# Interleaving two tensors: nine tiles of 28.5 KiB rows with three output buffers, in place of eight tiles of 32 KiB rows with two

## The chip, the core and the metric

The kernel runs on one core of a Trainium2 chip. A core has engines that run side by side, each with its own queue of instructions: here VectorE (DVE) copies, while SyncE (SP) and ScalarE (ACT) only issue DMA transfers. Sixteen DMA engines move data between the chip's large memory (HBM) and the core's own memory (SBUF), which has 128 partitions. Engines wait for one another by semaphores. The metric is the time of one execution on the device, in microseconds (us).

## The reference

```python
batch, seq, dim = 32, 256, 1024          # x, y: float32
result = np.zeros((batch, seq, dim * 2), dtype=np.float32)
result[..., 0::2] = x
result[..., 1::2] = y
```

The output takes its elements from x and y by turns. Nothing is computed: 33.55 MB of each input are read and 67.11 MB are written.

## The kernel before

The inputs are seen as flat arrays and cut into 8 tiles of 128 rows, each row 8192 float32 (32 KiB), one row to a partition. A tile of x and one of y give an output tile of 128 rows of 64 KiB; it is made and stored in two halves (h = 0 and 1), each 128 rows of 32 KiB. SBUF holds two buffers of x (xt), two of y (yt) and two for output halves (ot), all of 32 KiB a partition.

- *Loads* (L42 to L53) are issued by SP. The first tile of x comes as two halves with semaphores of their own (L42, L43), and these two DMAs are moved into the program's opening block, ahead of the common start (L103 to L122). Then come, tile by tile, x (L50) and y (L53). From the third tile on, the load of x waits (L48) until the third of the four copies of the tile two back is done, which is the last that reads that x buffer, and the load of y (L52) until the fourth is done.
- *Copies* (L55 to L70) are done by DVE, four a tile: for each half, x into the even places of the output buffer (L67), then y into the odd places (L70). The x copy waits for the tile's x and, from the second tile on, for the store that last used this output buffer (L64). The first y copy of a tile waits for y (L69). Each copy adds one to the semaphore `woven`.
- *Stores* (L72 to L85) are issued by ScalarE, each when its half has both copies. The first half is stored in two pieces, the first quarter (L77) and the rest (L81), all others as one DMA of 4096 KB (L83).
- *The end* (L87 to L93): ScalarE waits for the stores of output buffer 0 and clears the semaphores; SP waits for those of buffer 1, the last of which is the last store, and resets that semaphore.

Order is fixed by the program text on each of the three queues; between queues the semaphores alone decide. Loads and stores are separate DMA queues (q1 and q10 in the profile) that share the same sixteen engines.

Of the kernel before, what the change touches and what calls it, by code (L numbers as in the profile page):

```python
# [3 lines left out]


def _interleave(nc, x, y, out):
    P = 128
    W = 8192
    H = W // 2  # L10

    total = 1
    for s in x.shape:
        total *= s
    n = total // (P * W)
    assert n * P * W == total

    def rows(ap, names, k):
        flat = ap.rearrange("b s d -> (b s d)")
        return flat[k * names : (k + 1) * names].rearrange("(p w) -> p w", p=P)  # L20

    fp32 = mybir.dt.float32
    xt = [nc.alloc_sbuf_tensor(f"xt{b}", [P, W], fp32).ap() for b in (0, 1)]
    yt = [nc.alloc_sbuf_tensor(f"yt{b}", [P, W], fp32).ap() for b in (0, 1)]
    ot = [nc.alloc_sbuf_tensor(f"ot{b}", [P, W], fp32).ap() for b in (0, 1)]

    xsem = [nc.alloc_semaphore(f"xsem{b}") for b in (0, 1)]
    hsem = nc.alloc_semaphore("hsem")
    qsem = nc.alloc_semaphore("qsem")
    ysem = [nc.alloc_semaphore(f"ysem{b}") for b in (0, 1)]  # L30
    woven = nc.alloc_semaphore("woven")
    osem = [nc.alloc_semaphore(f"osem{b}") for b in (0, 1)]


    cuts = [0, W // 4, W]
    parts = [slice(a, b) for a, b in zip(cuts, cuts[1:])]

    xs = [rows(x, P * W, k) for k in range(n)]
    ys = [rows(y, P * W, k) for k in range(n)]
    os_ = [rows(out, 2 * P * W, k) for k in range(n)]  # L40

    nc.sync.dma_start(out=xt[0][:, :H], in_=xs[0][:, :H]).then_inc(xsem[0], 16)  # L42
    nc.sync.dma_start(out=xt[0][:, H:], in_=xs[0][:, H:]).then_inc(hsem, 16)  # L43

    for k in range(n):
        b = k % 2
        if k >= 2:
            nc.sync.wait_ge(woven, 4 * (k - 2) + 3)  # L48
        if k:
            nc.sync.dma_start(out=xt[b], in_=xs[k]).then_inc(xsem[b], 16)  # L50
        if k >= 2:
            nc.sync.wait_ge(woven, 4 * (k - 2) + 4)  # L52
        nc.sync.dma_start(out=yt[b], in_=ys[k]).then_inc(ysem[b], 16)  # L53

    for k in range(n):  # L55
        b = k % 2
        for h in (0, 1):
            c = slice(h * H, (h + 1) * H)
            if h == 0:
                nc.vector.wait_ge(xsem[b], 16 * (k // 2 + 1))  # L60
            elif k == 0:
                nc.vector.wait_ge(hsem, 16)
            if k:
                nc.vector.wait_ge(osem[h], 16 * k)  # L64
            if (k, h) == (1, 0):
                nc.vector.wait_ge(qsem, 16)
            nc.vector.tensor_copy(out=ot[h][:, 0::2], in_=xt[b][:, c]).then_inc(woven, 1)  # L67
            if h == 0:
                nc.vector.wait_ge(ysem[b], 16 * (k // 2 + 1))  # L69
            nc.vector.tensor_copy(out=ot[h][:, 1::2], in_=yt[b][:, c]).then_inc(woven, 1)  # L70

    for k in range(n):  # L72
        for h in (0, 1):
            nc.scalar.wait_ge(woven, 4 * k + 2 * h + 2)
            if (k, h) == (0, 0):
                for c in parts[:-1]:
                    nc.scalar.dma_start(  # L77
                        out=os_[k][:, c], in_=ot[h][:, c]
                    ).then_inc(qsem, 16)
                c = parts[-1]  # L80
                nc.scalar.dma_start(out=os_[k][:, c], in_=ot[h][:, c]).then_inc(osem[h], 16)  # L81
                continue
            nc.scalar.dma_start(  # L83
                out=os_[k][:, h * W : (h + 1) * W], in_=ot[h]
            ).then_inc(osem[h], 16)  # L85

    nc.scalar.wait_ge(osem[0], 16 * n)  # L87
    used = sorted(s.num for s in [*xsem, hsem, qsem, *ysem, woven, osem[0]])
    assert used == list(range(used[0], used[-1] + 1)), used
    nc.scalar.sem_clear(range(used[0], used[-1] + 1))  # L90
    nc.sync.nop(nofuse=True).wait_op(osem[1], 16 * n, "sem-ge").then_inc(
        osem[1], -16 * n
    )  # L93


def kernel(tc, x, y, out):
    nc = tc.nc
    tc.close()
    tc.compile()

    _interleave(nc, x, y, out)

    blocks = nc.main_func.blocks  # L103
    for engine in (mybir.EngineType.SP, mybir.EngineType.SP):
        opening = blocks[0].instructions
        at, moved = next(
            (b, i)
            for b in blocks[1:]
            for i in b.instructions
            if i.engine == engine and i.opcode == "DMACopy"  # L110
        )
        assert not (moved.sync_info and moved.sync_info.on_wait)
        body = at.instructions
        body.remove(moved)
        gate = next(
            n
            for n, i in enumerate(opening)
            if i.engine == engine and i.opcode == "Drain"
        )
        opening.insert(gate, moved)  # L120
        at.instructions = body
        blocks[0].instructions = opening  # L122


# [1 line left out]
_INS = ['x', 'y']  # L126
_OUTS = [((32, 256, 2048), 'float32')]


# [23 lines left out]
```

## Time and profile before

| what | us |
|---|---|
| time, median of 3 runs (314.10 to 314.26) | 314.18 |
| the profiled execution: span | 312.9 |
| DVE busy, 32 copies | 72.0 |
| one copy, 128x4096 | 2.29 |
| DVE waiting for stores | 206.5 |
| DVE waiting for y, once, and for x, once | 12.3 and 7.3 |
| store of 4096 KB, issue to landing, median | 34.1 |
| load of y, 4096 KB, issue to landing, median | 41.5 |

The span is the time from the first to the last event of one profiled execution, to which the other rows belong. The times of the runs are a little longer, since they hold what lies around the span; the span is 312.86 us in the trace, 1.32 us less than the median. Time to landing runs from the issuing instruction to the completion of the transfer, with all the time that it stands behind other transfers.

The profile names lines of the kernel (L67), engines (SPq and ACTq are the queues from which SP and ScalarE issue DMAs) and tiles without buffer numbers (ot for ot0 and ot1). A DMA packet is what one engine moves as one piece.

### The profile page before, as it was taken

The page shows a single profiled execution, that of the slowest core. Times are in us where ns is not written, and L with a number is a line of the kernel's source. Part 1 is how long each engine was busy: PE and PEld are TensorE (multiplying, and loading weights), DVE is VectorE, ACT ScalarE, POOL GpSimd, SP SyncE. Part 2 cuts the span into 40 slices and gives each one's busy share as a digit, 9 for nine tenths or more (in the row PEclk, how much of TensorE's full clock was granted, in tenths as well). Part 3 has the DMA queues.
Part 4 walks back from the last instruction along what each step waited for, and adds up shares of the span by engine and source line. Part 5 has one row for each costly group of instructions (what it writes and reads, how often), then busy time and mean ns, then how long its engine had stood idle before and what let it go on. Part 6 is the DMA issues. An engine that isn't in the chain of part 4 may idle for free.

```text
span 312.9 us, 114 instructions
## 1 busy us (share of the span) xinstructions
DVE 72.0 (23%) x32; POOL 0.2 (0%) x4
## 2 busy tenths in 40 slices
DVE  0216000501305023050220503205032050415410
POOL 0000000000000000000000000000000000000000
DMA  8999999999999999999999999999999999999998
GB/s 337 467 402 436 436 402 419 452 457 415 427 444 411 461 402 469 402 469 402 469 402 465 406 440 432 423 448 402 469 402 469 402 469 402 469 402 448 423 423 381
DMA packets 4896, 134.22 MB, mean 429 GB/s; under 512 B 544, under 2 KB 544, under 8 KB 544
## 3 DMA queue, kind: packets, MB, share of 16 engines
q1 hardware_dynamic: 2448, 67.11, 50.1%
q10 hardware_dynamic: 2448, 67.11, 49.7%
HBM read 67.11 MB, written 67.11 MB: 429 GB/s over the span
## 4 chain that ended last, share of the span: by engine, by line
DMA 82%; DVE 12%; issue 0%
DMA out_dram<-ot 76%; DMA yt<-in_y_dram 6%; DVE ot L70 6%; DVE ot L67 6%
## 5 line engine op out<-in xcount | busy, mean ns | idle before, releaser
L67 DVE COPY ot<-xt 128x4096 f32<-128x4096 f32 x16 | 36.7, 2295 | 213.8 <-DMA out_dram<-ot 206.5
L70 DVE COPY ot<-yt 128x4096 f32<-128x4096 f32 x16 | 36.6, 2288 | 12.3 <-DMA yt<-in_y_dram 12.3
L137 POOL MEMSET const-bfloat16-1.0<- 128x1 bf16 x1 | 0.1, 103 | 0.0
L137 POOL MEMSET const-uint8-127<- 128x1 uint8 x1 | 0.1, 102 | 0.0
L137 POOL MEMSET const-float32-0.0<- 128x1 f32 x1 | 0.1, 100 | 0.2 <-issue 0.2
L137 POOL MEMSET const-float32-1.0<- 128x1 f32 x1 | 0.1, 99 | 0.0
## 6 DMA issues: line engine op xcount, KB each, us to landing
out_dram<-ot ACTq DMA_DIRECT2D x15, 4096.0 KB, 34.1
yt<-in_y_dram SPq DMA_DIRECT2D x8, 4096.0 KB, 41.5
xt<-in_x_dram SPq DMA_DIRECT2D x7, 4096.0 KB, 24.3
xt<-in_x_dram SPq DMA_DIRECT2D x2, 2048.0 KB, 9.5
out_dram<-ot ACTq DMA_DIRECT2D x1, 3072.0 KB, 32.8
out_dram<-ot ACTq DMA_DIRECT2D x1, 1024.0 KB, 16.3
```

The lines of the kernel that those rows point to most:

```text
L67: nc.vector.tensor_copy(out=ot[h][:, 0::2], in_=xt[b][:, c]).then_inc(woven, 1)
L70: nc.vector.tensor_copy(out=ot[h][:, 1::2], in_=yt[b][:, c]).then_inc(woven, 1)
L137: nc = _bacc.Bacc("TRN2", target_bir_lowering=False, num_devices=1)
```

## The change

The tiles become nine: eight with rows of 7296 elements (28.5 KiB) and a ninth with rows of 7168 (28 KiB). The buffers have 28.5 KiB a partition; x and y keep two each, and the output has three. Output halves are numbered j = 2k + h over all tiles and use buffer j % 3, so a copy waits for the store three halves back (`osem[j % O]`) and not for the one two halves back. The first x load is still cut in two halves, now of 14592 bytes a row, and the first store in a quarter and the rest, now 7296 and 21888 bytes a row. The waits of the loads keep their counts. At the end ScalarE waits for the two output semaphores that don't belong to the last store, and SP for the third.

```diff
-    W = 8192
-    H = W // 2
+    WIDTHS = [7296] * 8 + [7168]
+    W = max(WIDTHS)
+    O = 3
...
-    ot = [nc.alloc_sbuf_tensor(f"ot{b}", [P, W], fp32).ap() for b in (0, 1)]
+    ot = [nc.alloc_sbuf_tensor(f"ot{b}", [P, W], fp32).ap() for b in range(O)]
...
+    half = WIDTHS[0] // 2
+    nc.sync.dma_start(out=xt[0][:, :half], in_=xs[0][:, :half]).then_inc(xsem[0], 16)
+    nc.sync.dma_start(out=xt[0][:, half : 2 * half], in_=xs[0][:, half:]).then_inc(hsem, 16)
...
-    for k in range(n):
+    for k, w in enumerate(WIDTHS):
         b = k % 2
         if k >= 2:
             nc.sync.wait_ge(woven, 4 * (k - 2) + 3)
         if k:
-            nc.sync.dma_start(out=xt[b], in_=xs[k]).then_inc(xsem[b], 16)
+            nc.sync.dma_start(out=xt[b][:, :w], in_=xs[k]).then_inc(xsem[b], 16)
...
+            j = 2 * k + h
+            c = slice(h * w // 2, (h + 1) * w // 2)
+            woven_to = ot[j % O]
             if h == 0:
                 nc.vector.wait_ge(xsem[b], 16 * (k // 2 + 1))
             elif k == 0:
                 nc.vector.wait_ge(hsem, 16)
-            if k:
-                nc.vector.wait_ge(osem[h], 16 * k)
-            if (k, h) == (1, 0):
+            if j >= O:
+                nc.vector.wait_ge(osem[j % O], 16 * (j // O))
+            if j == O:
                 nc.vector.wait_ge(qsem, 16)
-            nc.vector.tensor_copy(out=ot[h][:, 0::2], in_=xt[b][:, c]).then_inc(woven, 1)
+            nc.vector.tensor_copy(out=woven_to[:, 0:w:2], in_=xt[b][:, c]).then_inc(woven, 1)
             if h == 0:
                 nc.vector.wait_ge(ysem[b], 16 * (k // 2 + 1))
-            nc.vector.tensor_copy(out=ot[h][:, 1::2], in_=yt[b][:, c]).then_inc(woven, 1)
+            nc.vector.tensor_copy(out=woven_to[:, 1:w:2], in_=yt[b][:, c]).then_inc(woven, 1)
...
+            j = 2 * k + h
+            first = 0
+            nc.scalar.wait_ge(woven, 2 * j + 2)
+            if j == 0:
+                first = w // 4
+                nc.scalar.dma_start(out=os_[k][:, :first], in_=ot[0][:, :first]).then_inc(
+                    qsem, 16
+                )
             nc.scalar.dma_start(
-                out=os_[k][:, h * W : (h + 1) * W], in_=ot[h]
-            ).then_inc(osem[h], 16)
+                out=os_[k][:, h * w + first : (h + 1) * w], in_=ot[j % O][:, first:w]
+            ).then_inc(osem[j % O], 16)
...
+    for b in range(O):
+        if b != last:
+            nc.scalar.wait_ge(osem[b], done[b])
```

In the changed file, which is 10 lines longer, the x copy is L72, the y copy L75, the loads of x and y L53 and L56, and the stores L84 (the first quarter) and L87 (all others).

More of the change, by code (lines that the diff above doesn't have):

```diff
@@ L14, in _interleave, with tiles @@
         total *= s
-    n = total // (P * W)
-    assert n * P * W == total
-    def rows(ap, names, k):
+    n = len(WIDTHS)
+    assert sum(WIDTHS) * P == total
+    def tiles(ap, names):
         flat = ap.rearrange("b s d -> (b s d)")
-        return flat[k * names : (k + 1) * names].rearrange("(p w) -> p w", p=P)
+        cut, made = 0, []
+        for w in WIDTHS:
+            end = cut + names * P * w
+            made.append(flat[cut:end].rearrange("(p w) -> p w", p=P))
+            cut = end
+        return made
     fp32 = mybir.dt.float32
@@ L31, in _interleave @@
     woven = nc.alloc_semaphore("woven")
[L32 to L43, printed above, removed]
-    for k in range(n):
+    osem = [nc.alloc_semaphore(f"osem{b}") for b in range(O)]
+    xs = tiles(x, 1)
+    ys = tiles(y, 1)
+    os_ = tiles(out, 2)
+    half = WIDTHS[0] // 2
+    nc.sync.dma_start(out=xt[0][:, :half], in_=xs[0][:, :half]).then_inc(xsem[0], 16)
+    nc.sync.dma_start(out=xt[0][:, half : 2 * half], in_=xs[0][:, half:]).then_inc(hsem, 16)
+    for k, w in enumerate(WIDTHS):
         b = k % 2
@@ L69, in _interleave @@
                 nc.vector.wait_ge(ysem[b], 16 * (k // 2 + 1))
-            nc.vector.tensor_copy(out=ot[h][:, 1::2], in_=yt[b][:, c]).then_inc(woven, 1)
-    for k in range(n):
+            nc.vector.tensor_copy(out=woven_to[:, 1:w:2], in_=yt[b][:, c]).then_inc(woven, 1)
+    for k, w in enumerate(WIDTHS):
         for h in (0, 1):
[L74 to L82, printed above, removed]
-            nc.scalar.dma_start(
-                out=os_[k][:, h * W : (h + 1) * W], in_=ot[h]
-            ).then_inc(osem[h], 16)
@@ L87, in _interleave @@
-    nc.scalar.wait_ge(osem[0], 16 * n)
-    used = sorted(s.num for s in [*xsem, hsem, qsem, *ysem, woven, osem[0]])
+            j = 2 * k + h
[6 more added lines that the diff above has]
+                )
+            nc.scalar.dma_start(
+                out=os_[k][:, h * w + first : (h + 1) * w], in_=ot[j % O][:, first:w]
+            ).then_inc(osem[j % O], 16)
@@ L89, in _interleave @@
+    stores = 2 * n
+    last = (stores - 1) % O
+    done = [16 * len(range(b, stores, O)) for b in range(O)]
+    for b in range(O):
+        if b != last:
+            nc.scalar.wait_ge(osem[b], done[b])
+    clear = [s for b, s in enumerate(osem) if b != last]
+    used = sorted(s.num for s in [*xsem, hsem, qsem, *ysem, woven, *clear])
     assert used == list(range(used[0], used[-1] + 1)), used
     nc.scalar.sem_clear(range(used[0], used[-1] + 1))
-    nc.sync.nop(nofuse=True).wait_op(osem[1], 16 * n, "sem-ge").then_inc(
-        osem[1], -16 * n
+    nc.sync.nop(nofuse=True).wait_op(osem[last], done[last], "sem-ge").then_inc(
+        osem[last], -done[last]
```

5 lines of the change are left out of this document (2 added, 3 removed).

## The prediction

> **What bounds the kernel now.** I read the page's first three parts, then the chain of waits, the table of waits, the timeline, and last the windows by stage. DVE (VectorE) is the only compute engine in use, and it is not the bound:
>
> ```profile
> span 312.9 us, 114 instructions
> ...
> DVE 72.0 (23%) x32; POOL 0.2 (0%) x4
> ...
> DMA  8999999999999999999999999999999999999998
> ...
> DMA packets 4896, 134.22 MB, mean 429 GB/s; under 512 B 544, under 2 KB 544, under 8 KB 544
> ...
> q1 hardware_dynamic: 2448, 67.11, 50.1%
> q10 hardware_dynamic: 2448, 67.11, 49.7%
> ```
>
> The two queues' packets took 50.1% + 49.7% = 99.8% of the span on all sixteen DMA engines. So the engines are never idle between the first packet and the last one. The packet count also shows how a transfer is cut: 34 DMAs x 16 engines = 544 tiny completion packets, and the other 4352 are 34 x 128, one per row of a tile. So each engine does 8 row packets and one completion packet per DMA, 306 in all.
>
> ```profile
> DMA 82%; DVE 12%; issue 0%
> ```
>
> ```profile
> 81.36 34.17 DMA out_dram<-ot
> 115.53 0.02 issue
> 115.55 2.29 DVE ot L67
> 117.85 2.21 DVE ot L70
> 120.06 0.02 issue
> 120.08 34.17 DMA out_dram<-ot
> ```
>
> ```profile
> DVE ot L67 <- DMA out_dram<-ot: 206.5, 14, 29.0
> ```
>
> These are the page's chain, a stretch of the chain in order of time (start, length, what), and the first line of the waits (total, times, longest). DVE stood 206.5 us for output buffers, which a reader could take for a shortage of them. It is not: a store takes 34.17 us to land only because it shares full engines with the loads. The chain repeats every 120.08 - 81.36 = 38.72 us; windows over three such periods (length, DVE, POOL, clock, DMA share, GB/s) say what the engines do meanwhile:
>
> ```profile
> 41.00:79.70 38.70, 7.37 (x4) 0.00 (x0) 1.00 1.00 434
> ...
> 118.40:157.10 38.70, 8.97 (x5) 0.00 (x0) 1.00 1.00 434
> ...
> 195.80:234.60 38.80, 9.06 (x5) 0.00 (x0) 1.00 1.00 432
> ```
>
> The DMA share is 1.00 in each, at 432 to 434 GB/s. The end is as full, as the timeline's last copies but one show:
>
> ```profile
> 283.90 2.30 DVE L67 COPY ot<-xt 128x4096 f32<-128x4096 f32 x1 [8.95 <-DMA out_dram<-ot]
> ...
> 293.53 2.29 DVE L67 COPY ot<-xt 128x4096 f32<-128x4096 f32 x1 [5.14 <-DMA out_dram<-ot]
> ```
>
> Both copies were released by a store's landing, 9.63 us apart, with stores alone in flight: 4096 KB in 9.63 us is 435.5 GB/s. Loads mixed with stores and stores alone run at one rate.
>
> **What a packet costs.** The trace's single packet records, which the page only sums, took 309 ns for 8192 B, 611 for 16384, 912 for 24576 and 1213 for 32768: 301.3 ns for each 8 KiB, that is 27.2 GB/s per engine or 435 for sixteen, and a fixed part. The fixed part follows from the period: 38.72 us hold, per engine, 32 rows of 32 KiB (32 x 1205.2 = 38.57 us) and 36 packets in all, so 0.15 us / 36 = 4.2 ns a packet. The records' own remainder, 8 ns, is the upper bound, since records overlap a little. All bytes at 435 GB/s take 134.22 MB / 435 = 308.5 us, and 306 packets x 4.2 ns = 1.3 us: 309.8 of the 312.9 us. What is left, 3.1 us, is the first microsecond (16 GB/s in the window 0 to 1 us) and slow packets at two places: summed over an engine, 0.6 us in the first 3 us and 0.55 us between 26 and 41 us, when the first stores begin.
>
> **The change part by part.** The bytes stay. Everything else is counted against these 312.9 us and the 1.3 us by which the runs' median, 314.18 us, stands above this span; nothing in the change touches what lies outside the span, since SP's closing wait is still for the last store alone and ScalarE's wait for the other two output semaphores ends earlier.
>
> *More, shorter transfers.* Loads go from 17 to 19 and stores from 17 to 19: 38 DMAs, or 342 packets per engine instead of 306. The added 36 cost 36 x 4.2 ns = 0.15 us on the path, and at 8 ns 0.29 us. This is the one term that surely lands on the end.
>
> *Rows of 29184 B.* No packet of this size stands in the trace. By the line through the four sizes it takes 29184 / 8192 x 301.3 = 1073 ns plus the fixed part. All four sizes are multiples of 8 KiB, and this one is not, so the bounds are wide: below, the line (nothing extra, no reason for less); above, the full 1213 ns of the next size seen, 132 ns more for some 290 packets, 38 us. I take the line: from 8 to 32 KiB the fit is exact to 1 ns, which speaks for a cost by bytes and against one by steps of some other kind.
>
> *DVE's copies.* 36 instead of 32, of 3648 elements (the last four 3584): 2.29 us x 3648 / 4096 = 2.04 us each, 73 us in all. They are hidden by the DMA engines' queues; the question is only whether these ever run dry, which is the next term.
>
> *Two and two and three buffers.* SP's queue is released by the same counts (third and fourth copy of the tile two back), so a freed x or y buffer is reloaded at the same point of the tile. On DVE the wait for an output buffer is now for the store three back. Before, from a store's landing (76.83 us) to the next store's issue (81.36) two copies lie, 4.5 us, in which the other store and the loads kept the engines full. After, this gap is 4.1 us, and a further store of 3.74 MB can lie in the queue, 8.6 us alone. So cover grows, and DVE's 206.5 us of waiting shrinks or moves to the wait for y: as the stores get ahead, the copy held up is the one of L75 (y), with x already copied. Behind it in DVE's queue stands only what feeds the next store. Gain: none, as a DMA share of 1.00 cannot rise. Loss: none while anything is queued. An engine would idle only if all that is queued ended within two copies and the start of a transfer, 4.1 + 1.0 us (the first load's first bytes came 1 us after its issue), which is 5.1 x 0.435 = 2.2 MB; while DVE waits for y, the two other output buffers are stored, up to 7.5 MB.
>
> *Start and end.* Five loads are still issued in the first 3.2 us; they now carry 14.9 MB instead of 16.8, 34 us of work, and the first store follows the first y, which landed at 21.9 us and now needs a ninth less. The end is two stores after the last copy; store 17's copies take 4 us beside store 16 of 8.4 us. Taken as zero.
>
> Sum: 312.86 + 0.15 = 313.0 us of span, + 1.32 = 314.33 us.
>
> **The rivals.** A difference of 0.2%, 0.63 us, is about what a measurement of this kernel can tell from no change.
>
> *Rows cost more (slower).* Place: each of the some 300 data packets of an engine. For it: the untested size, and the first pieces with rows odder still (7296 and 21888 B of the first store, 14592 B of the first loads). Against it: the fit to 1 ns. It decides from (0.63 - 0.15) / 304 = 1.6 ns a packet. A row moved as two packets would add a fixed part to each, 304 x 4.2 ns = 1.3 us: 315.6 us. Rows charged by whole KiB (29 instead of 28.5) would add 0.5 x 301.3 / 8 = 19 ns to some 290: 5.5 us, 319.8 us.
>
> *The queues run dry at the last y (slower).* With three output buffers the stores can catch up with the loads, whose buffers got smaller; if stores 14 and 15 are done when the last y lands, the engines stand for one copy and a start, 2.04 + 1.0 us: 317.4 us. For it: DVE's waits move to y. Against it: the last load was issued at 236.26 us and loads of y take 41.5 us, so it landed near 278, 35 us before the end; nine smaller tiles shorten this lead by a ninth at most, and a third buffer by one store's time, to some 22 us, of which stores 16 and 17 are 17.
>
> *Each added DMA pays a fixed cost in line (slower).* If the start of a transfer, the first 1.0 us, were a gap on the engines at each of the four added DMAs, it would be 4.0 us: 318.3 us. Against it: 9.63 us for 4096 KB alone, which leaves no such gap between two stores. The page "DMA: Bandwidth & Descriptors" of the Trainium skill, in "Anatomy of one DMA", has the stronger form: each DMA (there, one issued from GpSimd) takes about 2.0 us plus its bytes at 436 GB/s. By that the four would be 8 us, an estimate from the page, if nothing overlapped; the trace disagrees, since a store would then take 11.6 us where 9.63 were seen.
>
> *The slow packets vanish (faster).* Another pitch of the rows or a different overlap at the first stores could save the 0.6 + 0.55 us of slow packets: 314.33 - 1.15 = 313.2 us. For it: they are the only time above the line. Against it: both come with a first use (first loads, first stores), which stays. [...]
>
> *The third buffer does not do what it is there for.* This is the forecast: DVE waits less for stores and nothing ends earlier.
>
> **How the numbers follow.** Forecast, no change that shows: 0.66. Rows cost more: 0.16. Dry at the end: 0.05. In-line cost: 0.02. Slow packets vanish: 0.08, and 0.03 for a gain from something the trace doesn't show. Slower by over 0.2%: 0.16 + 0.05 + 0.02 = 0.23; faster: 0.11; within: 0.66. The likeliest case gives 314.33 us, on its own 314.1 to 314.8. The range reaches to 313.5 us on the low side (a little over half of the slow packets saved) and to 315.9 on the high side (a second fixed part per row); the rest of the slower cases and the largest gain, under 2 in 10, are left out.
>
> **What would show it.** The page should have 5472 packets, 608 of them under 512 B, a DMA share near 99.8%, and 434 GB/s in the middle. The waits of DVE should be fewer for stores and more for y, and the copies near 2.04 us. Rows that cost more show as packets longer than 1081 ns and a lower rate in each slice; a dry queue as a slice under 9 or a DMA share under 1.00 late; a gain as fewer slow packets in the first 41 us. The prediction falls if the middle runs at another rate than 432 to 435 GB/s.

## The result, and the profile after

The changed kernel takes 315.0 us (median of 16 runs, 314.76 to 315.79) beside 314.24 us of the kernel before (16 runs on the same chip, 314.10 to 314.46). The ratio is 1.0028, 95% interval 1.0022 to 1.0035: slower by some 0.8 us. (The ratios in this text go by the means of the runs; where the runs spread unevenly they differ a little from the ratio of the medians.) It is not only later but less steady: its runs spread over 1.0 us, those of the kernel before over 0.4.

The page of the changed kernel, in the lines that answer to those of before:

```profile
span 314.2 us, 124 instructions
...
DVE 73.2 (23%) x36; POOL 0.2 (0%) x4
...
DMA  8999999999999999999999999999999999999997
...
DMA packets 5472, 134.22 MB, mean 427 GB/s; under 512 B 608, under 2 KB 608, under 8 KB 736
...
q1 hardware_dynamic: 2736, 67.11, 50.0%
q10 hardware_dynamic: 2736, 67.11, 49.5%
```

There are 5472 packets, 342 for each engine. The two shares now add up to 99.5% where they were 99.8%, and the last slice is a 7. The waits of DVE (total, times, longest):

```profile
DVE ot L72 <- DMA out_dram<-ot: 156.5, 15, 13.3
DVE ot L75 <- DMA yt<-in_y_dram: 51.7, 9, 11.1
```

DVE waits 50 us less for output buffers and 39 us more for y (12.3 us before): the third buffer does what it should to DVE, and the wait moves to the next input. The middle of the run did not change. Windows over two periods of the changed kernel (length, DVE, POOL, clock, DMA share, GB/s):

```profile
138.50:173.00 34.50, 8.15 (x4) 0.00 (x0) 1.00 1.00 433
173.00:207.50 34.50, 8.15 (x4) 0.00 (x0) 1.00 1.00 433
```

So the time is lost neither between transfers nor in the rows of the middle: the packet records of 29184 B took 1081 ns, which is 29184 / 8192 x 301.3 + 8, the line through the four sizes of before. It shows at the very end. Short windows of the changed kernel; a packet's bytes are counted where the packet starts:

```profile
311.30:311.80 0.50, 0.00 (x0) 0.00 (x0) 1.00 2.12 918
311.80:312.60 0.80, 0.00 (x0) 0.00 (x0) 1.00 0.01 0
312.60:312.90 0.30, 0.00 (x0) 0.00 (x0) 1.00 0.23 96
312.90:314.20 1.30, 0.00 (x0) 0.00 (x0) 1.00 0.00 0
```

And of the kernel before:

```profile
310.80:311.30 0.50, 0.00 (x0) 0.00 (x0) 1.00 2.43 1049
311.30:312.40 1.10, 0.00 (x0) 0.00 (x0) 1.00 0.01 0
```

Read them as packets. Before, 1049 GB/s x 0.5 us = 524 KB is sixteen rows of 32 KiB: all sixteen engines start their last row within half a microsecond, and nothing starts afterwards. After, 918 x 0.5 = 459 KB is sixteen rows of 28 KiB; then, almost 1 us later, 96 x 0.3 = 29 KB: one more row, on one engine. The whole kernel waits for this engine while fifteen are done. (The trace does not number the engines. It shows them as sixteen chains of packets, each packet starting within a few ns of the end of the one before.)

The completion packets, sixteen for each DMA, say how this came about. The table gives, in us from the start of the span, the mean over the sixteen engines of their last completion, the last engine's, what engines lost to slow packets (records above the line, summed over an engine, mean), and the spread of the sixteen completions of the very first load. Medians are over all runs; the first profile of the changed kernel is of a run of 315.5 us, the second of one of 315.05.

| kernel | median | span | mean end | last engine | slow packets | spread, first load |
|---|---|---|---|---|---|---|
| before | 314.24 | 312.86 | 312.35 | 312.48 | 1.18 | 0.40 |
| changed, first profile | 315.0 | 314.18 | 312.65 | 313.80 | 1.44 | 0.89 |
| changed, second profile | 315.05 | 313.73 | 312.89 | 313.35 | 1.68 | 0.57 |

In the first profile the engines' mean moved by 0.30 us: 0.15 of added packets, 0.26 of slow packets, and 0.13 less because the engines started a little earlier. The other 1.02 us of the 1.32 us of longer span are the last engine's distance from the mean, 1.15 us where it was 0.13. In the second profile, whose run took the median, it is more slow packets (+0.50), added packets (0.15), less for the start (0.13), and the last engine's distance (+0.33).

The late engine was late from its first rows. It started 0.6 us after most others (at 1.75 us; the other fifteen between 1.00 and 1.32), and its first packet was as slow as theirs (1.18 us, theirs 0.94 to 1.48, where 0.55 is usual). At the first load's completion it was 0.44 us behind the next engine, at y of tile 0, near 20 us, 0.59, at x of tile 1 0.92, at the end 0.97 us. In between, while loads and stores share the engines, its distance stands in the loads, 1.84 us at 59 us and 2.05 from 93 us on, after two packets that were 0.2 us slow at 86 us, and hardly in the stores (0.1 us); with stores alone it is 0.97. Each engine has its fixed eight rows of each DMA, so an engine that has fallen behind stays behind: engines that are never idle cannot be caught up.

### The profile page after: what moved, and what is told of

It reads as the page before. It is cut to its first block, busy times and chain, and to the rows that moved or that the text cites. A ratio compares the mean times of both kernels' runs of the same rounds, so it can differ in the third digit from the quotient of the medians.

```text
span 314.2 us, 124 instructions
## 1 busy us (share of the span) xinstructions
DVE 73.2 (23%) x36; POOL 0.2 (0%) x4
## 2 busy tenths in 40 slices
DMA packets 5472, 134.22 MB, mean 427 GB/s; under 512 B 608, under 2 KB 608, under 8 KB 736
## 4 chain that ended last, share of the span: by engine, by line
DMA 82%; DVE 7%; another core or an unknown queue 3%; SPq 0%; issue 0%; DVEq 0%
DMA out_dram<-ot 69%; DMA yt<-in_y_dram 13%; DVE ot L75 4%; DVE ot L72 3%; SPq L53 0%; SPq L56 0%; DVEq L69 0%
## 5 line engine op out<-in xcount | busy, mean ns | idle before, releaser
L72 DVE COPY ot<-xt 128x3648 f32<-128x3648 f32 (+1 forms) x18 | 37.0, 2057 | 167.7 <-DMA out_dram<-ot 156.5
L75 DVE COPY ot<-yt 128x3648 f32<-128x3648 f32 (+1 forms) x18 | 37.0, 2054 | 51.7 <-DMA yt<-in_y_dram 51.7
```

The lines of the kernel that those rows point to most:

```text
L72: nc.vector.tensor_copy(out=woven_to[:, 0:w:2], in_=xt[b][:, c]).then_inc(woven, 1)
L75: nc.vector.tensor_copy(out=woven_to[:, 1:w:2], in_=yt[b][:, c]).then_inc(woven, 1)
```

## The experiments

All times are compared with runs of the kernel before on the same chip in the same session; its medians there lay between 314.17 and 314.24 us, and none of its runs above 314.48.

### The changed kernel again, and with two output buffers

> The changed kernel once more, for a second profile and more times. Theory A (the extra over the 0.15 us of added packets is one DMA engine that falls behind in the first 40 us, as the first profile shows: 15 engines end within 0.38 us of each other and one 0.97 us later): the median is again 0.6 to 0.9 us above before, the runs again spread over about 1 us, and the profile again has an engine that ends late, by another amount. Rival B (the first profile's late engine is an accident, the extra lies in the steady middle): the spread over engines is 0.4 us and the middle period is longer than 34.5 us.

Measured: 315.05 us (314.76 to 315.91), ratio 1.0032 (1.0022 to 1.0042). The spread is there, and another picture of it: no single engine, but sixteen ends from 312.45 to 313.35 us (windows as above):

```profile
311.20:311.80 0.60, 0.00 (x0) 0.00 (x0) 1.00 1.00 430
311.80:312.40 0.60, 0.00 (x0) 0.00 (x0) 1.00 0.89 382
312.40:312.90 0.50, 0.00 (x0) 0.00 (x0) 1.00 0.01 0
```

Rival B falls: the middle runs at 433 GB/s here too, with the same period of 34.51 us. Theory A holds only in a wider form: the engines fall apart and the last one counts, but not all of it comes early. Of the 0.50 us of added slow packets 0.31 lie after 41 us, most of them thirteen rows of a load that start between 68.3 and 68.9 us and take up to 0.49 us too long. In the first profile only 0.03 us lie after 41 us.

```diff
-    O = 3
+    O = 2
```

> The nine tiles with two output buffers in place of three: the tile part of the change alone. Theory A (late engine at the start): same as the changed kernel, +0.6 to +0.9 us over before, since the first 40 us are almost the same. Rival C (the third buffer's queue of stores costs the time): +0.15 us over before, 314.4 us.

Measured: 315.0 us (314.79 to 315.65), ratio 1.0027 (1.0018 to 1.0037), with engines' ends from 312.36 to 313.26 us. The third buffer neither gains nor costs anything that can be measured; the tiles make the difference.

### Which rows make engines fall behind

```diff
-    WIDTHS = [7296] * 8 + [7168]
+    WIDTHS = [7168] + [7296] * 8
```

> The nine tiles with the 28 KiB tile first, so that the first x halves are 14336 B a row and the first store's pieces 7168 and 21504 B, all whole KiB; the rest is as in the changed kernel. Theory D (the odd pieces of the first DMAs make an engine fall behind): +0.15 to +0.3 us over before, and runs within 0.4 us. Theory E (every row of 28.5 KiB, or the start of rows off large powers of two, disturbs the start): still +0.6 to +0.9 us.

Measured: 314.76 us (314.61 to 315.86), ratio 1.0023 (1.0014 to 1.0032). Nine of eleven runs lie between 314.61 and 315.06, two at 315.8. The profile was taken on one of the bad ones, and its end shows a single engine again, still more clearly (windows as above):

```profile
311.20:311.80 0.60, 0.00 (x0) 0.00 (x0) 1.00 1.69 730
311.80:312.40 0.60, 0.00 (x0) 0.00 (x0) 1.00 0.11 49
312.40:313.00 0.60, 0.00 (x0) 0.00 (x0) 1.00 0.01 0
313.00:313.60 0.60, 0.00 (x0) 0.00 (x0) 1.00 0.11 49
```

49 GB/s x 0.6 us is one row, started after 313.0 us when the other engines had stopped. From 53 us to the end the last engine's completion comes 1.35 us after the next one's in each of the 32 DMAs, loads and stores: nothing is made up. First pieces of whole KiB do not prevent the late engine, so theory D in its simple form falls; theory E's size, 0.6 to 0.9 us, is just missed by the median (0.54).

The kernel before with only its first pieces cut as in the changed kernel:

```diff
+    X = 3648
...
-    cuts = [0, W // 4, W]
+    cuts = [0, 1824, W]
...
-    nc.sync.dma_start(out=xt[0][:, :H], in_=xs[0][:, :H]).then_inc(xsem[0], 16)
-    nc.sync.dma_start(out=xt[0][:, H:], in_=xs[0][:, H:]).then_inc(hsem, 16)
+    nc.sync.dma_start(out=xt[0][:, :X], in_=xs[0][:, :X]).then_inc(xsem[0], 16)
+    nc.sync.dma_start(out=xt[0][:, X:], in_=xs[0][:, X:]).then_inc(hsem, 16)
...
-            elif k == 0:
+            if k == 0 and h == 0:
```

> The kernel before, eight tiles of 32 KiB rows, but its first x load cut into rows of 14592 and 18176 B and its first store into 7296 and 25472 B. Theory D (odd first pieces): +0.4 to +0.7 us over before, with runs spread over 1 us. Theory E: as before, within 0.1 us.

Measured: 314.57 us (314.24 to 315.36), ratio 1.0016 (1.0007 to 1.0024). So a part of the change that adds not one packet brings part of the loss, and the spread. (The second piece takes the rest of the row, and the first copy waits for both pieces, as also in odd_load and uneven_load.) The two cuts alone:

> The kernel before with only its first x load cut oddly, rows of 14592 and 18176 B in place of twice 16384. If the spread of odd_head comes from the first loads: median +0.2 to +0.4 us over before, runs spread over 1 us. If from the first store: as before, within 0.4 us.

> The kernel before with only its first store cut oddly, rows of 7296 and 25472 B in place of 8192 and 24576. If the spread of odd_head comes from the first store: median +0.2 to +0.4 us over before, runs spread over 1 us. If from the first loads: as before, within 0.4 us.

Measured: with the load's cut alone 315.11 us (314.22 to 315.39), ratio 1.0021 (1.0013 to 1.0030); with the store's alone 314.30 us (314.15 to 314.42), ratio 1.0002 (0.9993 to 1.0010). So it is the first load's cut, or the wait that goes with it. That wait was not tried alone; it moves DVE's first copy from 7.33 to 12.42 us, but the first copy of y starts as before when y has landed, at 22.05 us (21.91 before). The runs fall into two groups: three of eleven from 314.22 to 314.46, as before, and eight from 314.80 to 315.39. The profile caught one of the first group: its engines ended within 0.33 us of each other, and its span was 312.9 us. The late group was therefore not seen in a trace of this kernel. In odd_head, with the same load, six of eleven runs lie above all runs of before; which group holds the median is partly chance.

```diff
+    X = 3072
...
-    nc.sync.dma_start(out=xt[0][:, :H], in_=xs[0][:, :H]).then_inc(xsem[0], 16)
-    nc.sync.dma_start(out=xt[0][:, H:], in_=xs[0][:, H:]).then_inc(hsem, 16)
+    nc.sync.dma_start(out=xt[0][:, :X], in_=xs[0][:, :X]).then_inc(xsem[0], 16)
+    nc.sync.dma_start(out=xt[0][:, X:], in_=xs[0][:, X:]).then_inc(hsem, 16)
...
-            elif k == 0:
+            if k == 0 and h == 0:
```

> The kernel before with its first x load cut into rows of 12288 and 20480 B in place of twice 16384; the rows' pitch stays 32 KiB; as in odd_load the first copy waits for both pieces. If only odd lengths (14592 B, no multiple of 1 KiB) make the late engine: as before, within 0.1 us, runs within 0.4 us. If any cut but two times 16 KiB does: median +0.3 to +0.9 us, runs spread over 1 us, as in odd_load.

Measured: 314.31 us (314.21 to 315.23), ratio 1.0009 (1.0001 to 1.0018): eight of eleven runs as before, three from 315.05 to 315.23. Neither expectation held; the cut into unequal pieces of whole KiB has late runs too, but fewer, though 3 against 8 of eleven runs is not a clear difference. The profile is of a run as before, so whether an engine was late in the three is not shown. The copy waits as in odd_load, and here most runs are as before, so the wait alone does not make late runs frequent.

```diff
-    half = WIDTHS[0] // 2
+    half = 4096
...
-    nc.sync.dma_start(out=xt[0][:, half : 2 * half], in_=xs[0][:, half:]).then_inc(hsem, 16)
+    nc.sync.dma_start(out=xt[0][:, half : WIDTHS[0]], in_=xs[0][:, half:]).then_inc(hsem, 16)
```

> The changed kernel with its first x load cut at 16384 B (then 12800 B) in place of twice 14592 B; the rows' pitch stays 29184 B. If the length of the first rows makes the late engine: +0.15 to +0.3 us over before, runs within 0.4 us. If it is the pitch of the rows in HBM: unchanged, +0.6 to +0.9 us.

Measured: 315.86 us (314.96 to 316.03, five runs), ratio 1.0049 (1.0036 to 1.0061), the slowest of the nine-tile kernels. The first rows are 16384 B long, as in the kernel before, but 29184 B apart. One engine completed its part of this load 0.99 us after the next one (the sixteen were 1.37 us apart). This engine's first packet starts at 2.93 us, where the others start between 0.98 and 1.87 us, so it is late before it has moved a row; it completes last in every DMA, to the end, 1.23 us after the next. It is seen on the page of waits too: DVE's first copy, which waits for just this load, starts at 8.18 us, in the kernel before at 7.33, with rows of the same length. The timeline of this kernel:

```profile
8.18 2.06 DVE L72 COPY ot<-xt 128x3648 f32<-128x3648 f32 x1 [8.18 <-DMA xt<-in_x_dram]
```

So the length of the first rows alone is not the cause. Tiles of 28 KiB and of 16 KiB rows, with larger numbers of DMAs:

```diff
-    WIDTHS = [7296] * 8 + [7168]
+    WIDTHS = [7168] * 9 + [1024]
...
+    osem = [osem[0], osem[2], osem[1]]
```

> Nine tiles with 28 KiB rows and a tenth with 4 KiB rows, two, two and three buffers: 42 DMAs, 378 packets per engine, so +0.3 us from the packets, and 128 small rows at the end. Theory F (rows that start off the 4 KiB grid are what makes engines fall behind): 314.5 us with runs within 0.4 us. Theory G (any first rows other than the 32 KiB tile's do, or the order of the first transfers): median 0.6 to 1.0 us over before and runs spread over 1 us.

(The second line only gives two output semaphores each other's number, as the last store now uses buffer 1.) Measured: 315.41 us (315.28 to 316.35, five runs), ratio 1.0042 (1.0029 to 1.0054). The packets account for 0.3 us of the 1.2; the profile, of the 316.35 us run, has its last engine 1.34 us after the mean. Rows on a grid of 4 KiB do not help: theory F falls.

```diff
-    W = 8192
+    W = 4096
```

> The kernel before with tiles of half the row (16 KiB rows, 16 tiles, everything else the same): 66 DMAs instead of 34, so 594 packets per engine instead of 306. The packet term of the prediction (4.2 ns a packet) gives 288 x 4.2 ns = 1.2 us, 315.4 us; by 8 ns 2.3 us, 316.5 us; a cost of 1 us per added DMA in line would give 32 us. If the spread comes from rows off the 8 KiB grid, the runs here stay within 0.4 us.

Measured: 316.71 us (316.35 to 317.26, five runs), ratio 1.0082 (1.0069 to 1.0096), more than 4.2 ns a packet gives. The trace takes the 2.44 us of longer span apart: the engines' mean end is 314.15 us, 1.80 later, of which 288 x 4.2 ns = 1.2 are packets and 0.39 are slow packets; the last engine is 0.78 us after the mean instead of 0.13, another 0.65; about 0.2 are left over. The period (36 packets, 32 of them rows of 16 KiB) is 19.449 us, 4.6 ns a packet above the bytes. The packet term is about right, and engines fall apart here too, with rows that are powers of two.

### The same first 40 us

```diff
-    WIDTHS = [7296] * 8 + [7168]
+    WIDTHS = [8192] + [7168] * 8
...
-    O = 3
+    O = 2
```

> Nine tiles again, 38 DMAs, but the first with rows of 32 KiB and eight of 28 KiB, two output buffers: the first x load (rows of 16384 B twice), the first y and the first store are exactly those of the kernel before. Theory H (the late engine is made by the first load, by its rows not being 16 KiB long at a pitch of 32): only the packets are left, +0.15 to +0.25 us over before, 314.4 us, runs within 0.4 us, first landing of x spread over the engines by 0.4 to 0.5 us as before. Theory I (the other tiles' rows or the larger number of tiles make it): +0.5 to +0.9 us and runs spread over 1 us.

Measured: 314.88 us (314.53 to 315.07), ratio 1.0021 (1.0012 to 1.0030). Theory H failed, in an instructive way; the size is theory I's, the spread of the runs, 0.54 us, is not. The first load completed on all engines within 0.39 us, as before, and no run shows the large delays; but at x of tile 1, in flight when the first stores begin (packets from 27.7 us), the engines were 0.94 us apart, where the kernel before has 0.35. Slow packets cost 1.43 us instead of 1.18. So there is a second place where engines fall apart: the loads that run beside the first stores. The rows of 28 KiB begin at the same place, with tile 1; this run does not part the two.

```diff
-    WIDTHS = [7296] * 8 + [7168]
+    WIDTHS = [8192] * 7 + [4096] * 2
...
-    O = 3
+    O = 2
```

> Nine tiles and 38 DMAs, 342 packets per engine as in the changed kernel, but seven tiles of 32 KiB rows and then two of 16 KiB, two output buffers: all that moves in the first 40 us is what the kernel before moves. Theory J (the extra beyond the packets is made in the first 40 us, where engines fall behind, and kept to the end): only the packets are left, +0.1 to +0.25 us over before, 314.3 to 314.45 us, runs within 0.4 us, the engines' ends within 0.3 us. Theory K (nine tiles or 38 DMAs cost it as such): +0.5 to +0.9 us.

Measured: 314.40 us (314.27 to 314.68), ratio 1.0007 (0.9998 to 1.0016). Nine tiles, 38 DMAs and 5472 packets, exactly as many as in the changed kernel, cost 0.2 us when the first 40 us are those of the kernel before, and the interval still holds no change at all. From its page:

```profile
span 313.1 us, 123 instructions
...
DMA packets 5472, 134.22 MB, mean 429 GB/s; under 512 B 608, under 2 KB 608, under 8 KB 608
...
q1 hardware_dynamic: 2736, 67.11, 50.1%
q10 hardware_dynamic: 2736, 67.11, 49.7%
```

and its end, in windows:

```profile
311.80:312.40 0.60, 0.00 (x0) 0.00 (x0) 1.00 0.77 328
312.40:313.20 0.80, 0.00 (x0) 0.00 (x0) 1.00 0.01 0
```

The share is back at 99.8%, and no engine starts a row alone after the others. Mean end 312.50 us, last engine 312.72: beside the kernel before, 0.15 us of packets, as the prediction had them, and 0.09 of spread (the ends lie 0.40 us apart, where theory J had 0.3). Theory K falls. J fits, but is not shown by this kernel alone, which keeps not only the first 40 us but also rows of 32 KiB in seven tiles; the traces of the changed kernel bear J out for the most part in the first profile, and in the second less.

## Why the prediction was right and wrong

**Right: what bounds the kernel.** In windows of one period (34.5 us) the middle of the changed kernel runs at 432 to 435 GB/s, and of two_out at 431 to 433, with a DMA share of 1.00 or 1.01. The third buffer is worth nothing, as two_out shows, since DVE's wait was never the limit.

**Right: the packets.** 36 more packets per engine were put at 0.15 us. tail_cut, which adds only these, moved the engines' mean end by 0.15 us and the median by 0.2. In small_tiles, with 288 more, the period gives 4.6 ns a packet, and the changed kernel's own period of 34.51 us gives 4.4.

**Right: the rows.** The line through multiples of 8 KiB also holds for 29184, 28672, 21888 and 7296 B: 1081, 1062, 813 and 276 ns. The rival "rows cost more" falls; its price, 315.6 us, is near the measured time by accident. That the measured 315.0 us lies within the range is luck too: the likeliest case ended at 314.8 us, and the upper end was drawn for this rival.

**Right: DVE and the queues.** Copies of 2.06 us for 2.04; the waits moved to y; no queue ran dry (once all engines run, each packet of the changed kernel starts within 4 ns of another's end), so that rival falls. So does the one of a fixed cost in line: four more DMAs cost 0.2 us in tail_cut, not 4.

**Wrong: "Start and end ... Taken as zero".** This is the step that failed, and with it the likeliest case: within 0.2% had 0.66, and the kernel became slower by 0.28%. Two things were missing. First, the sum treated the sixteen engines as one. It worked with means (share of busy time, GB/s, slow packets summed over an engine), but the end is the end of the slowest engine. In the kernel before the two are the same within 0.13 us, so the profile gave little sign of it; after, they differ by 0.46 and 1.15 us in two profiles. The prediction's own account had a gap here: of the 3.1 us that it gave to the start and the slow packets, it named 1.0 + 0.6 + 0.55. In that trace, most of the other 0.9 is 0.3 us by which the engines on the mean start after the first one, 0.13 us from their mean end to the last, and 0.38 us from there to the end of the span. Second, the slow packets were allowed to vanish, which became the faster rival, and never to grow or to fall unevenly. "Both come with a first use (first loads, first stores), which stays" was true and not enough: slow packets cost 1.18 us before, and 1.44 and 1.68 with the new tiles. No gain was forecast, and there was none. Of the 0.8 us lost, the added packets are some 0.2; the rest goes with the rows of the tiles. In the first profile most of it is there by 41 us; in the second 0.31 us of slow packets come later, most of them at 68 us, a place that the prediction did not have.

**Two smaller slips.** The range's low end, 313.5 us, would need 0.83 of the 1.15 us of slow packets, nearer three quarters than "a little over half". And a difference of 0.2% is not the least that can be told: the interval of the result is 0.13% wide.

**Open: why.** What in the first transfers makes engines fall behind was not found. Length of the first rows, whole KiB, powers of two, and the first store's pieces are excluded as the sole cause. No run of the kernel before, with rows 32 KiB apart and the first tile in two equal halves, lay above 314.48 us; odd_store, which has the same loads, stayed as low, and tail_cut's runs went to 314.68. head32 has the same first load, but rows of 28 KiB after it, and fell apart at the first stores. Every other first load that was tried had late runs, or engines that ended far apart. What made the packets at 68 us slow is open too.

## What to carry to other kernels

When transfers bound a kernel and their engines are full, more buffers buy nothing; ask only what the change does to packets and to the first and last microseconds. Work that is split over engines in fixed shares ends with the slowest: look at how far apart the engines complete, not at the mean share. And a layout tried out on a kernel like this one can be tried by its first load: cheap experiments that keep the first 40 us and change the rest, or the other way round, tell the two apart, as long as nothing else changes with them.

## What the runs showed of the hardware

- A DMA engine that is behind stays behind to the end: in even_head the last engine completes 1.35 us after the next in each of the 32 DMAs that land from 53 to 314 us.
- The cut of one load of 4 MB among 134 MB, with the wait of its copy, moved the median by 0.9 us and put its runs in two groups (314.22 to 314.46 and 314.80 to 315.39 us).
- Queued DMAs follow each other without a gap (in the kernel before the sixteen chains of packets have one, of 0.05 us at 2.3 us); only the packets count. The periods with rows of 16, 28.5 and 32 KiB give 4.6, 4.4 and 4.2 ns a packet beside 301.3 ns per 8 KiB, and the single records of rows from 7296 B to 32 KiB lie on one line.
- An engine takes rows of the two queues by turns, whatever their size: while the first piece of a store (rows of 8 KiB) and a load (rows of 32 KiB) ran together in the kernel before (28.7 to 39.9 us), one row of each alternated on an engine.
